# One core, two blocks: the first block's output stage by halves of the tokens, and a new order of products in every half block of weights

## The chip, the cores and the metric

The kernel runs on one core of a Trainium2 chip. The metric is the device time of one execution in microseconds (us), the median of several executions. Five engines work side by side, each through an order of instructions of its own that is fixed when the kernel is built: TensorE (PE in the profile, its weight loads apart as PEld), VectorE (DVE), ScalarE (ACT), GpSimd (POOL) and SyncE (SP), which issues the DMAs.

## The reference, cut to what matters

`x` holds 512 tokens of 2048 channels. A first block (convolution, attention, gates) ends in an output product, a norm and a residual; a second block starts with a norm, a modulation by a vector, and a wide product:

```python
# first block, its end
out = merged @ w_o                                   # 2048 x 2048
x = x + gate * rms_norm(out, g_post)
# second block, its start
h = rmsnorm(x, norm_g) * (1.0 + scale) + shift
u = h @ w_in                                         # 68 blocks of 128 columns, as the kernel lays them out
```

`u` feeds a gated delta network (8 heads) and an RWKV mixer. The same `w_in` is also applied to 256 context tokens, whose mixers run earlier.

## The kernel before

**Layout.** Activations are kept with channels on the partitions: 16 tiles of 128 channels x 512 tokens. A weight block is 128 output columns over 16 slices of 128 input channels. For precision, each operand is held as a pair hi + lo in fp32r (`split`, L104: ACT casts to hi at L105, DVE subtracts at L106 to get lo), and a product of two pairs is three matmuls: hi·hi, hi·lo and lo·hi, the first factor being the weight.

**Products.** `mblock` (L132) makes one block of 128 columns for T tokens in a PSUM bank: it calls `products` (L141) for each half block of 8 slices. `products` loads a half block of weights (512 KB, three buffers `wraw`), splits it into `whi` and `wlo` (two buffers each), and issues 24 matmuls at L157. For each slice k in turn it issues whi·act_hi, whi·act_lo, wlo·act_hi. Four slices instead of eight are taken where tiles of the activation become ready bit by bit.

**Order.** A scheduler puts the instructions of each engine in order when the kernel is built, by their place in the program (the priority) and by when its own model of time has them ready. Within `products`, groups of `K.burst` matmuls (12, later 6) are kept together.

**The output stage** (L1470 to L1491, in `block1`). 16 blocks of `wo` for all 512 tokens; each is scaled out of PSUM by DVE (L1470, tiles `out0` to `out15`), squared by ACT, and the squares are summed by POOL (`ChanSS` with `pe=False`). Then `rinv` sums over the partitions with two matmuls and computes an inverse root in 11 DVE operations (`rsqrt`, L161 to L175). Each of the 16 tiles is scaled by it (L1478, DVE), x is added (L1479, DVE for every third tile, POOL for the others), the sum is stored to DRAM (L1480) and its squares are summed by PE (L290). A second `rinv` follows, and then `modulate_steps` (L335) makes the pairs `h` tile by tile. As soon as four tiles are there, `products` goes through the same four slices of three blocks of the second block's weights (`K.pre`, blocks `B_LO` to `B_LO+2`; `PRE = 3`), which stay in three PSUM banks (`px0`, `px1`, one `pc`). `mixers_gdn` then takes the fourth such block by `mblock` (bank `pd`) and starts the heads.

**Other users of `products`.** The context stage runs `mblock` with T = 256 (tiles `hc`); there POOL makes every second `wlo` (`K.on_pool = 2`). The eight heads of the delta network in `mixers_gdn` take four blocks each with T = 512, `K.burst` = 6.

Of the kernel before, what the change touches and what calls it, by code (L numbers as in the profile page):

```python
# [9 lines left out]
F32 = mybir.dt.float32  # L10
# [3 lines left out]
ALU = mybir.AluOpType  # L14
# [41 lines left out]
PRE = 3  # L56
# [55 lines left out]
class Visit:  # L112
# [6 lines left out]
    def mm(self, *a, **kw):  # L119
# [5 lines left out]
        if self.first:  # L125
            tc.add_manual_dep(i, self.first.name, mybir.DependencyInfo(mybir.DependencyClass.NoSync,
                                                                       mybir.DependencyReason.DATA), reason="visit")
        else:
            self.first = i
# [11 lines left out]
def products(K, ps, wap, act, T, ka, w, k0, k1):  # L141
# [9 lines left out]
    for k in range(w):  # L151
        ah, al = act[k]
        for j, (a, b) in enumerate(((hi, ah), (hi, al), (lo, ah))):
            n = 3 * (ka - k0 + k) + j
            ahead = FIRST if n % K.burst else 0
            tc.cur_priority -= ahead
            nc.tensor.matmul(ps[:, :T], lhsT=a[:, k], rhs=b, start=(n == 0), stop=(n == 3 * (k1 - k0) - 1))  # L157
            tc.cur_priority += ahead
# [1248 lines left out]
def block1(K, h, big, late, cc):  # L1407
# [31 lines left out]
    with left(K, "ext", 16) as ext:  # L1439
# [21 lines left out]
        with right(K, "ot") as op:  # L1461
            K.x1d = K.dram.tile([16, 128, 512], F32, name="x1d")
            outs = []
            ss = ChanSS(K, op, 512, 16, "or", False)
            gg = op.tile([128, 16], F32, name="gg")
            nc.vector.tensor_tensor(gg, K.mod["ada"][:, 32:48, 0], K.v["g_post"], op=ALU.mult)
# [9 lines left out]
            for i in range(16):  # L1476
                x, o = xs[i], outs[i]
                nc.vector.tensor_tensor(o, o, ro, op=ALU.mult)  # L1478
                (nc.gpsimd if i % 3 else nc.vector).tensor_tensor(o, o, x, op=ALU.add)  # L1479
                K.dma.dma_start(K.x1d[i], o)  # L1480
                s2.add(o)
# [365 lines left out]
```

## Time and profile before

| what | value |
|---|---|
| median of 3 executions | 3961.03 us (3956.98 to 3964.54) |
| profiled execution: time | 3948.75 us |
| profiled execution: span | 3947.0 us |
| mean granted TensorE clock in it | 0.962 of full speed |
| PE busy | 3672.7 us (93%) |
| DVE busy | 2748.4 us (70%) |
| ACT busy | 1359.4 us (34%) |
| POOL busy | 505.4 us (13%) |

Times in the rows are us from the start of the span. The busy time of PE counts matmuls that overlap in the pipeline, so where PE is busy all the time its rate is read from the distance between starts.

### The profile page before, as it was taken

What the parts mean: (1) busy time and instruction counts of PE and PEld (TensorE: products, weight loads), DVE (VectorE), ACT (ScalarE), POOL (GpSimd) and SP (SyncE); (2) the same over time, 40 slices, a digit from 0 to 9 for tenths busy, and PEclk for the clock granted to TensorE, in tenths of its full rate; (3) what the DMA queues carried; (4) which work ended last, traced back from release to release, by engine and by line L of the source; (5) the groups of instructions that cost most, each with busy time, mean ns of one, the idle gap of its engine ahead of it and who ended that gap; (6) DMA issues with size and microseconds to landing.
All of it is one profiled execution on the core that took longest, in us unless ns stands there. A gap on an engine that the chain in (4) does not pass through costs nothing. (4 is left out here: it accounts for less than half of the span.)

```text
span 3947.0 us, 81802 instructions
## 1 busy us (share of the span) xinstructions
PE 3672.7 (93%) x33066; PEld 2837.3 (72%) x33066; DVE 2748.4 (70%) x7146; ACT 1359.4 (34%) x2713; POOL 505.4 (13%) x595
## 2 busy tenths in 40 slices
PE   8899878999999999999998889989999999998997
PEld 4577678876777777777886577777877777766676
DVE  3366798788778778553524877776767778877866
ACT  3322333323334344332322432322323444444333
POOL 0100231003101001000311201100001111111102
PEclk9999899999999999999999999999999999999998
DMA  8766445423433333425523222222223122212235
GB/s 321 269 226 216 161 133 173 140 102 127 136 118 107 118 111 126 130 81 179 204 93 129 101 88 68 67 69 75 86 79 110 65 68 81 68 67 83 91 129 203
DMA packets 206491, 492.95 MB, mean 125 GB/s; under 512 B 40096, under 2 KB 71328, under 8 KB 202016
## 3 DMA queue, kind: packets, MB, share of 16 engines
q1 hardware_dynamic: 206112, 487.72, 36.4%
q8 instruction: 260, 4.26, 0.4%
q14 instruction: 119, 0.97, 0.1%
HBM read 434.54 MB, written 53.09 MB: 124 GB/s over the span
## 5 line engine op out<-in xcount | busy, mean ns | idle before, releaser
L157 PE MATMUL pd<-big,whi 128*128 128x512 f32 x5280 | 1759.5, 411 | 8.0 <-ACT big L352 8.0
L157 PEld LDWEIGHTS pd<-big,whi 128*128 128x128 f32 x5280 | 964.4, 192 | 251.4 <-issue 20.8
L157 PE MATMUL pd<-big,wlo 128*128 128x512 f32 x2768 | 1104.2, 399 | 24.3 <-DVE wlo L106 23.6
L105 ACT CAST whi<-wraw 128x1024 fp32r<-128x1024 f32 (+2 forms) x498 | 502.9, 1010 | 1159.5 <-PE pd L157 1074.7
L106 DVE TENSOR_TENSOR wlo<-wraw,whi 128x1024 fp32r<-128x1024 f32 (+2 forms) x478 | 572.9, 1199 | 318.4 <-ACT whi L105 311.2
L157 PEld LDWEIGHTS pd<-big,wlo 128*128 128x128 f32 x2768 | 530.0, 191 | 147.1 <-DVE wlo L106 28.2
L157 PE MATMUL pd<-hc,whi 128*128 128x256 f32 x1152 | 227.0, 297 | 11.5 <-ACT hc L352 5.5
L157 PE MATMUL pd<-hc,wlo 128*128 128x256 f32 x576 | 171.7, 298 | 33.0 <-DVE wlo L106 23.9
L157 PEld LDWEIGHTS pd<-hc,whi 128*128 128x128 f32 x1152 | 188.3, 199 | 15.3 <-ACT hc L352 5.6
L157 PE MATMUL pd<-ext,whi 128*128 128x512 f32 x512 | 184.6, 401 | 3.8 <-DVE ext L106 3.8
L1160 DVE SCALAR_TENSOR_TENSOR cv_y<-cv_up,vec,cv_y 128x512 f32<-128x512 f32 x240 | 180.9, 754 | 4.2
L157 PE MATMUL pd<-fa,whi 128*128 128x512 f32 x448 | 149.9, 414 | 0.9 <-ACT fa L105 0.8
L157 PEld LDWEIGHTS pd<-hc,wlo 128*128 128x128 f32 x576 | 114.8, 199 | 40.0 <-DVE wlo L106 28.0
L944 POOL TENSOR_TENSOR rg_bk<-rg_th,rg_L 64x512 f32<-64x512 f32 x48 | 69.1, 1439 | 400.5 <-ACT rg_L L923 274.0
L1055 ACT ACTIVATE rg_zw<-rg_H,rg_wc 64x64 f32<-64x64 f32 x320 | 102.8, 342 | 43.4 <-DVE rg_H L1077 39.2
L157 PEld LDWEIGHTS pd<-ext,whi 128*128 128x128 f32 x512 | 97.3, 190 | 27.9 <-DVE ext L106 4.7
L1077 DVE SCALAR_TENSOR_TENSOR rg_H<-pc,rg_wc,rg_zw 64x64 f32<-64x64 f32 x320 | 90.4, 282 | 33.7 <-PE pc L123 24.0
L567 DVE SCALAR_TENSOR_TENSOR gc_y<-gc_up,vec,gc_y 128x512 f32<-128x512 f32 (+1 forms) x160 | 108.6, 679 | 2.8 <-issue 0.2
L242 DVE SCALAR_TENSOR_TENSOR ada_ev<-wraw,cs_ada,ada_ev 128x512 f32<-128x512 f32 x120 | 93.7, 781 | 20.3 <-DMA wraw<-in_wada_dram 18.9
L157 PEld LDWEIGHTS pd<-fa,whi 128*128 128x128 f32 x448 | 80.7, 190 | 21.8 <-ACT fa L105 1.9
L157 PE MATMUL pd<-fa,wlo 128*128 128x512 f32 x224 | 89.1, 398 | 0.7 <-DVE wlo L106 0.7
L405 DVE COPY_PREDICATED iv_u<-cpi,px 128x256 f32<-128x256 int32 (+2 forms) x112 | 35.2, 340 | 73.2 <-PE px L402 62.8
(589 smaller groups left out, 5592.9 us busy)
## 6 DMA issues: line engine op xcount, KB each, us to landing
wraw<-in_w_dram SPq DMA_DIRECT2D x366, 512.0 KB, 3.6
wraw<-in_wada_dram SPq DMA_DIRECT2D x128, 512.0 KB, 4.5
wraw<-in_wada_dram SPq DMA_DIRECT2D x32, 1024.0 KB, 4.8
wraw<-in_wo_dram SPq DMA_DIRECT2D x32, 512.0 KB, 3.5
sgl<-sgd SPq DMA_DIRECT2D x48, 256.0 KB, 3.3
wraw<-in_wout_dram SPq DMA_DIRECT2D x20, 512.0 KB, 3.8
wraw<-in_w_dram SPq DMA_DIRECT2D x36, 256.0 KB, 3.6
sgd<-msg SPq DMA_DIRECT2D x32, 256.0 KB, 3.3
```

Of the source, the lines that this page charges most:

```text
L105: K.nc.scalar.copy(hi, src)
L106: (eng or K.nc.vector).tensor_tensor(lo, src, hi.bitcast(F32), op=ALU.subtract)
L157: nc.tensor.matmul(ps[:, :T], lhsT=a[:, k], rhs=b, start=(n == 0), stop=(n == 3 * (k1 - k0) - 1))
L242: nc.vector.scalar_tensor_tensor(ev, raw[:, k], cs[:, kk, 0:1], ev, op0=ALU.mult, op1=ALU.add)
L405: nc.vector.copy_predicated(u32[:, m0:m0 + w], K.cp[d, lev].unsqueeze(1).to_broadcast([128, w, 32]), zp[:, m0:m0 + w])
L567: nc.vector.scalar_tensor_tensor(y, up[:, t:t + T], w[:, t:t + 1], y, op0=ALU.mult, op1=ALU.add)
L944: nc.gpsimd.tensor_tensor(bk[uq, :, u], th[uq], F[uq], op=mul)
L1055: nc.scalar.activation(zw[hv[u], d], H[hv[u], ms[d], u], AF.Copy, scale=wn[hv[u], 4 * d + mn])
L1077: nc.vector.scalar_tensor_tensor(Hn[hv[u], 4 * d + mn, u], pc3[hv[u], 2, d], wn[hv[u], 4 * d + mn], zw[hv[u], d], op0=mul, op1=ALU.add)
L1160: nc.vector.scalar_tensor_tensor(y, up[:, t:t + 512], w[:, t:t + 1], y, op0=ALU.mult, op1=ALU.add)
```

## The change

Four things are changed.

- `products` issues, for a half block, first all whi·act_hi and whi·act_lo of its slices, and then all wlo·act_hi. This holds for every product of the kernel that goes through it.
- The output stage becomes a function of its own, `block1_out`, that works on tokens 0 to 255 and then on tokens 256 to 511. The `wo` products of the first half come first; their norm, residual, second norm and modulation (`norms(0)`) are spread over the `wo` products of the second half, three steps per block. The squares of the second norm are summed by POOL in the first half and by PE in the second; x is loaded in halves with three buffers.
- `PRE` falls away: four blocks instead of three are begun ahead, each in two halves of 256 columns of its bank. The first halves of all four are issued with the steps of `norms(1)` between them, and the second halves follow the modulation of the second half of the tokens.
- A dependency without a wait (`behind`) keeps the second half of a bank after its first half. `Visit` uses the same helper, with no other effect.

All weights of `wo` and of the four blocks are loaded and split twice, once for each half. The hi part of `h` takes the place of the hi part of the merged activations.

```diff
-PRE = 3
...
-def products(K, ps, wap, act, T, ka, w, k0, k1):
+def products(K, ps, wap, act, T, ka, w, k0, k1, after=None):
...
-    for k in range(w):
-        ah, al = act[k]
-        for j, (a, b) in enumerate(((hi, ah), (hi, al), (lo, ah))):
-            n = 3 * (ka - k0 + k) + j
-            ahead = FIRST if n % K.burst else 0
-            tc.cur_priority -= ahead
-            nc.tensor.matmul(ps[:, :T], lhsT=a[:, k], rhs=b, start=(n == 0), stop=(n == 3 * (k1 - k0) - 1))
-            tc.cur_priority += ahead
+    n = 3 * (ka - k0)
+
+    for a, k, b in [(hi, k, b) for k in range(w) for b in act[k]] + [(lo, k, act[k][0]) for k in range(w)]:
+        ahead = FIRST if n % K.burst else 0
+        tc.cur_priority -= ahead
+        i = nc.tensor.matmul(ps[:, :T], lhsT=a[:, k], rhs=b, start=(n == 0), stop=(n == 3 * (k1 - k0) - 1)).ins
+        tc.cur_priority += ahead
+        if after:
+            behind(K, i, after)
+            after = None
+        n += 1
+    return i
...
-            outs = []
-            ss = ChanSS(K, op, 512, 16, "or", False)
...
-            for i in range(16):
-                o = op.tile([128, 512], F32, name=f"out{i}")
-                ps = mblock(K, A["wo"][i], m, 512)
-                nc.vector.tensor_scalar(o, ps, gg[:, i:i + 1], None, op0=ALU.mult)
-                ss.add(ps)
-                outs.append(o)
-            ro = ss.rinv(1.0 / 2048, EPS)
-            s2 = ChanSS(K, op, 512, 16, "or")
-            xs = [loader(K, ext, A["xT"], 512, "ext", 16)(i) for i in range(16)]
...
-            for m in modulate_steps(K, op, lambda k: outs[k], pair_of(big, "big"), r2, 512, "ng2", "ada2", 0, "or"):
-                h.append(m)
-                k = len(h) - 4
-                if k % 4 == 0:
-                    for b, ps in K.pre.items():
-                        products(K, ps, A["w2"][b], h[k:], 512, k, 4, 0, 16)
-            return h
+            return block1_out(K, big, op, m)
+
+
+def block1_out(K, big, op, m):
...
+    outs = [op.tile([128, 512], F32, name=f"out{i}") for i in range(16)]
+    h = [(hi, big.tile([128, 512], F32R, name="big")) for hi, _ in m]
+    hs = [slice(0, 256), slice(256, 512)]
+
+    def wo(t, sums):
+        act = [[x[:, hs[t]] for x in pair] for pair in m]
+        for i in range(16):
+            ps = mblock(K, A["wo"][i], act, 256)
+            nc.vector.tensor_scalar(outs[i][:, hs[t]], ps, gg[:, i:i + 1], None, op0=ALU.mult)
+            sums.add(ps)
+            yield
+
+    def norms(t, sums):
+        ro = sums.rinv(1.0 / 2048, EPS)
+        s2 = ChanSS(K, op, 256, 16, "os", t == 1)
+        get = loader(K, op, A["xT"][:, :, hs[t]], 256, "or_x", 3)
+        yield
+        for i in range(16):
+            x, o = get(i), outs[i][:, hs[t]]
+            nc.vector.tensor_tensor(o, o, ro, op=ALU.mult)
+            (nc.gpsimd if i % 3 else nc.vector).tensor_tensor(o, o, x, op=ALU.add)
+            K.dma.dma_start(K.x1d[i][:, hs[t]], o)
+            s2.add(o)
+            yield
+        r2 = s2.rinv(1.0 / 2048, EPS)
+        yield
+        it = iter(h)
+        yield from modulate_steps(K, op, lambda k: outs[k][:, hs[t]], lambda: [x[:, hs[t]] for x in next(it)], r2, 256,
+                                  "ng2", "ada2", 0, "om")
+
+    sums = ChanSS(K, op, 256, 16, "or", False)
+    run(wo(0, sums))
+    first = norms(0, sums)
+    run(first, 1)
+    sums = ChanSS(K, op, 256, 16, "or", False)
+    for _ in wo(1, sums):
+        run(first, 3)
+    run(first)
+    K.pre = {B_LO + j: p.tile([128, 512], F32, name=n) for j, (p, n) in
+             enumerate(((K.px, "px0"), (K.px, "px1"), (K.pc, "pc"), (K.pc, "pc")))}
+    other = norms(1, sums)
+    done = {}
+
+    def begin(t, k):
+        act = [[x[:, hs[t]] for x in pair] for pair in h[k:k + 4]]
+        for b, ps in K.pre.items():
+            done[b] = products(K, ps[:, hs[t]], A["w2"][b], act, 256, k, 4, 0, 16, done[b] if t and not k else None)
+            if not t:
+                run(other, 1)
+
+    for k in range(0, 16, 4):
+        begin(0, k)
+    run(other, 2)
+    for k in range(0, 16, 4):
+        run(other, 4)
+        begin(1, k)
+    return h
```

## Rows read from the trace of the kernel before

**Rows 1.** The page: busy time of PE, DVE, ACT and POOL in the span.
```profile
PE 3672.7 (93%) x33066; PEld 2837.3 (72%) x33066; DVE 2748.4 (70%) x7146; ACT 1359.4 (34%) x2713; POOL 505.4 (13%) x595
```
**Rows 2.** Stretches: length, busy (count) of PE PEld DVE ACT POOL, clock, DMA, GB/s.
```profile
1969.00:2147.00 178.00, 178.00 (x770) 144.39 (x769) 52.34 (x57) 43.04 (x49) 25.41 (x15) 1.00 0.30 104
2147.00:2194.00 47.00, 20.04 (x35) 5.67 (x34) 41.99 (x48) 11.90 (x19) 18.19 (x11) 0.81 0.34 127
2194.00:2235.00 41.00, 38.62 (x144) 28.91 (x144) 30.40 (x39) 24.69 (x39) 11.18 (x7) 0.89 0.25 88
2235.00:2247.00 12.00, 11.35 (x49) 8.94 (x49) 11.17 (x16) 4.62 (x7) 0.00 (x0) 1.00 0.50 159
```
**Rows 3.** Timeline of PE: first and last `wo` product, first of the second block.
```profile
1968.81 0.39 PE L157 MATMUL pd<-big,whi 128*128 128x512 f32 x1
...
2146.07 0.39 PE L157 MATMUL pd<-big,wlo 128*128 128x512 f32 x1
...
2194.24 1.58 PE L157 MATMUL px<-big,whi 128*128 128x512 f32 x2 [11.15 <-ACT big L352]
```
**Rows 4.** Timeline of DVE: first operations of norm, scaling, second norm, modulation.
```profile
2149.16 0.69 DVE L168 TENSOR_SCALAR or_xh<-po 128x512 f32<-128x512 f32 x1 [1.31 <-PE po L294]
...
2156.89 1.29 DVE L1478 TENSOR_TENSOR out<-out,or_y 128x512 f32<-128x512 f32 x2
...
2183.13 0.69 DVE L168 TENSOR_SCALAR or_xh<-po 128x512 f32<-128x512 f32 x1 [2.19 <-PE po L290]
...
2190.85 2.42 DVE L351 SCALAR_TENSOR_TENSOR or_n<-out,or_gs,or_y 128x512 f32<-128x512 f32 x2
```
**Rows 5.** Timeline of PE, context stage, 256 columns: two starts, 90 products apart.
```profile
639.15 0.28 PE L157 MATMUL pd<-hc,wlo 128*128 128x256 f32 x1
...
649.80 0.28 PE L157 MATMUL pd<-hc,wlo 128*128 128x256 f32 x1
```
**Rows 6.** Groups of instructions, 1975 to 2147: busy, mean ns, idle before.
```profile
L106 DVE TENSOR_TENSOR wlo<-wraw,whi 128x1024 fp32r<-128x1024 f32 x30 | 36.8, 1226 | 63.9 <-ACT whi L105 62.4
L105 ACT CAST whi<-wraw 128x1024 fp32r<-128x1024 f32 x30 | 31.5, 1049 | 123.3 <-PE pd L157 123.3
```
**Rows 7.** Groups of instructions, 2147 to 2220.
```profile
L1478 DVE TENSOR_TENSOR out<-out,or_y 128x512 f32<-128x512 f32 x16 | 19.8, 1283 | 0.0
...
L1479 POOL TENSOR_TENSOR out<-out,ext 128x512 f32<-128x512 f32 x10 | 16.4, 1643 | 25.3 <-DVE out L1478 25.3
...
L106 DVE TENSOR_TENSOR wlo<-wraw,whi 128x512 fp32r<-128x512 f32 x6 | 5.2, 863 | 0.1
```
**Rows 8.** Groups of instructions of 256 columns, 440 to 740 (context stage).
```profile
L173 DVE SCALAR_TENSOR_TENSOR gn_t<-gn_y 128x256 f32<-128x256 f32 x16 | 6.7, 418 | 0.0
...
L347 POOL TENSOR_TENSOR hc_n<-cr_in,c_ri 128x256 f32<-128x256 f32 x7 | 6.2, 883 | 7.6 <-DVE hc L353 7.6
```
**Rows 9.** Waits of PE, 440 to 740: us in total, times, longest.
```profile
PE pd L157 <- DVE wlo L106: 23.9, 16, 4.3
PE pd L157 <- POOL wlo L106: 8.8, 14, 2.0
```
**Rows 10.** A stretch of the context stage, columns as in rows 2.
```profile
548.00:628.00 80.00, 64.44 (x496) 60.53 (x497) 69.04 (x118) 28.45 (x45) 23.92 (x29) 1.00 0.44 150
```
**Rows 11.** Waits of PE, 2396 to 2792 (heads of the delta network).
```profile
PE pd L157 <- DVE wlo L106: 22.6, 5, 4.5
```
**Rows 12.** Timeline of PE around one of these five waits.
```profile
2489.27 0.73 PE L157 MATMUL pd<-big,whi 128*128 128x512 f32 x2
2494.51 0.80 PE L157 MATMUL pd<-big,wlo 128*128 128x512 f32 x1 [4.51 <-DVE wlo L106]
...
2495.96 0.63 PE L157 MATMUL pd<-big,wlo 128*128 128x512 f32 x1
...
2499.80 0.63 PE L157 MATMUL pd<-big,wlo 128*128 128x512 f32 x1
```
**Rows 13.** The stretch of that head, columns as in rows 2.
```profile
2475.00:2555.00 80.00, 74.15 (x765) 60.10 (x764) 58.71 (x184) 23.09 (x42) 8.47 (x21) 0.96 0.21 69
```

More of the change, by code (lines that the diff above doesn't have):

```diff
@@ L125, in mm @@
         if self.first:
-            tc.add_manual_dep(i, self.first.name, mybir.DependencyInfo(mybir.DependencyClass.NoSync,
-                                                                       mybir.DependencyReason.DATA), reason="visit")
+            behind(self.K, i, self.first, "visit")
         else:
@@ L150, in products, with behind @@
     split(K, hi[:, :w], lo[:, :w], raw[:, :w], nc.gpsimd if K.on_pool and K.n_split % K.on_pool == 0 else nc.vector)
-    for k in range(w):
-        ah, al = act[k]
-        for j, (a, b) in enumerate(((hi, ah), (hi, al), (lo, ah))):
-            n = 3 * (ka - k0 + k) + j
-            ahead = FIRST if n % K.burst else 0
-            tc.cur_priority -= ahead
-            nc.tensor.matmul(ps[:, :T], lhsT=a[:, k], rhs=b, start=(n == 0), stop=(n == 3 * (k1 - k0) - 1))
-            tc.cur_priority += ahead
+    n = 3 * (ka - k0)
[9 more added lines that the diff above has]
+    return i
+def behind(K, i, first, reason="order"):
+    K.tc.add_manual_dep(i, first.name, mybir.DependencyInfo(mybir.DependencyClass.NoSync, mybir.DependencyReason.DATA),
+                        reason=reason)
 def rsqrt(K, pool, src, shape, a, eps, name, eng=None, exact=False):
@@ L1473, in block1 @@
-            ro = ss.rinv(1.0 / 2048, EPS)
-            s2 = ChanSS(K, op, 512, 16, "or")
-            xs = [loader(K, ext, A["xT"], 512, "ext", 16)(i) for i in range(16)]
[L1476 to L1481, printed above, removed]
-            r2 = s2.rinv(1.0 / 2048, EPS)
@@ L1483, in block1 @@
-            K.pre = {B_LO + j: p.tile([128, 512], F32, name=n) for j, (p, n) in
-                     enumerate(((K.px, "px0"), (K.px, "px1"), (K.pc, "pc"), (K.pc, "pc"))[:PRE])}
-            h = []
-            for m in modulate_steps(K, op, lambda k: outs[k], pair_of(big, "big"), r2, 512, "ng2", "ada2", 0, "or"):
-                h.append(m)
-                k = len(h) - 4
-                if k % 4 == 0:
-                    for b, ps in K.pre.items():
-                        products(K, ps, A["w2"][b], h[k:], 512, k, 4, 0, 16)
@@ L1492, in block1 @@
-            return h
+            return block1_out(K, big, op, m)
+def block1_out(K, big, op, m):
+    nc, A = K.nc, K.A
+    K.x1d = K.dram.tile([16, 128, 512], F32, name="x1d")
+    gg = op.tile([128, 16], F32, name="gg")
+    nc.vector.tensor_tensor(gg, K.mod["ada"][:, 32:48, 0], K.v["g_post"], op=ALU.mult)
+    outs = [op.tile([128, 512], F32, name=f"out{i}") for i in range(16)]
[50 more added lines that the diff above has]
+    return h
```

3 lines of the change are left out of this document (removed).

## The prediction, made before the changed kernel was run

> **What bounds the kernel now.** I read the page first. PE is busy for 93% of the span, DVE for 70% [rows 1], so only what removes idle or slow time of PE can move the end. The next view was the table of stretches around the output stage [rows 2]. From 1969 to 2147 PE is busy without a gap at full clock. In the 47 us behind it, PE runs 35 matmuls, and DVE is busy for 42.0 us: a chain on DVE sets the pace. In the next 41 us, 144 products of the second block pass, at a mean clock of 0.89, and 12 us later the fourth low-rank block is done. The timelines say which links the chain has: the last `wo` product starts at 2146.07 and the first product of the second block at 2194.24, after a wait for the modulated tile [rows 3]. Between them DVE starts the first inverse root at 2149.16, the scaling at 2156.89, the second root at 2183.13 and the modulation at 2190.85 [rows 4].
>
> The view of waits says where else PE waits for what the change touches. In the context stage it waits 30 times, 32.7 us in all, for a low weight product's operand [rows 9]. In the heads it waits five times, 4.5 us each [rows 11]. One of these in the timeline [rows 12]: two whi products at 2489.27, then nothing until `wlo` is there at 2494.51. The nine products from 2495.96 to 2499.80 start 0.427 us apart, nearly twice the 0.231 us of [rows 3] (177.26 us over 767 intervals). [...]
>
> **Part 1, the halved `wo` products.** 768 products of 512 columns become 1536 of 256. In the context stage 256 columns cost 10.65 us for 90 products, 0.118 us each [rows 5]. 1536 x 0.1183 = 181.7 us against 768 x 0.2311 = 177.5 us: **+4 us**.
>
> Weight loads as the limit: each matmul in [rows 2] has a load of its own (770 and 769), and in [rows 5] a product with its load starts every 0.118 us, so the load is hidden at 256 columns too. [...]
>
> The weights must come twice as fast: one half block per 24 x 0.118 = 2.84 us. The cast takes 1.05 us and the subtraction 1.23 us [rows 6], in sequence 2.3, so both fit. With the old order the `whi` buffer would be held almost to the end of the 24 products; with hi first it is free after 16 of them (0.95 us earlier), and `wlo` is wanted 1.7 us later (14 products). That is what keeps a half block fed at 2.84 us.
>
> The second half of `wo` (90.9 us) also carries `norms(0)`. DVE's work in it: 32 subtractions x 1.226 = 39.2 us, 16 evictions = 7 us (an estimate, 0.6 of their 512-column time), two roots of 11 x 0.42 us = 9.2 us [rows 8], 22 scalings and additions of 0.4 us = 9 us, and the modulation, 11 us (an estimate from the root's 0.42 us per operation): 76 us. POOL has 28 sums of squares, 10 additions and 8 scalings of 0.88 us [rows 8], 41 us. Below, nothing: 76 < 91. Above: DVE and POOL hold each other up, since the scaling takes 1.283 us in the mean beside POOL's additions [rows 7] where DVE's root needs 0.70 us per operation [rows 4]. If they took turns throughout, 76 + 41 = 117 us, 26 us over. SP's queue is in order as well: 16 loads of x (three buffers, so each waits for an addition three tiles back) and 16 stores now stand between weight loads, and a late addition delays the weights behind it. I take **+10 us**, nearer the low end because the three weight buffers lie ahead; range 0 to 26.
>
> **Part 2, what follows `wo`.** Before: from 2146.07 to 2247, when four low-rank blocks are done, 101 us. After, only the second half's chain follows, with 256 columns. DVE's 256-column operation takes 0.418 us [rows 8] against 0.70: ratio 0.6; POOL's 0.883 against 1.643 us [rows 7]: 0.54. Up to the first root 3.1 us become 2.5. The root, 7.7 us, becomes 4.7. Scaling, addition and the sum of squares, 26.2 us, become 15. The second root 4.7. The modulation with the second halves of the products: PE needs 192 x 0.118 = 22.7 us, DVE some 12 us of modulation and 16 subtractions of 0.69 to 0.86 us [rows 7]; I take 28. Sum 55. Meanwhile the first halves of the four blocks (22.7 us of PE work) cover the chain; their 16 subtractions (11 to 14 us) share DVE with it: +7. Total 62 us. Lower bound: PE's work alone, 45.4 us plus 16 sums, 52. Upper: all 14 us of subtractions in the way and a half-clock start, 73. Gain **39 us**, range 28 to 49. This is also the cover of Part 1: the first half's norm and modulation cost nothing because 91 us of products run over them; without that cover they cost what the second half's do, some 40 us.
>
> **Part 3, low products last, elsewhere.** Context stage: `wlo` is wanted 14 x 0.118 = 1.7 us later and `whi` is free 0.95 us earlier, against a mean wait of 32.7/30 = 1.1 us. By that nearly all 32.7 us go. But in a stretch where PE is busy for 64.4 of 80 us, DVE is for 69.0 [rows 10]: it can be shortened by no more than 11 us before DVE is the limit, and it is in order. I take **-10 us**, range 0 to 33.
>
> [...] I take **-20 us**, range 0 to 35.
>
> The rest of the kernel shows PE waits for `wlo` of under 1 us each, so no gain; but the scheduler lays the whole order out anew. I price that at 0, with 12 us to either side, the size of the profiled run's distance from the median. The fourth bank (`pc`) is held until the low-rank step reads it, as the other three are: 0.
>
> **Sum.** +4 + 10 - 39 - 10 - 20 = -55 us. Against the profiled time, 3948.75 - 55 = 3894. That run lies 12.3 us below the median, so the median should be 3906; I say **3907 us**.
>
> **The rivals.**
> - *Only the order gains.* `wo`'s second half is paced by DVE and POOL (+26) and the chain ends at its upper bound (-28): +2 with the 4 us. Then 3961 - 30 + 2 = 3933. For it: DVE's 42.0 of 47 us [rows 2]. Against it: nine tenths of that chain move under products that run anyway. 0.12.
> - *Only the halves gain.* DVE sets the pace in the context stage and the heads, so the waits only move: 3961 - 25 = 3936. For it: [rows 10]. Against it: [rows 13]. 0.07.
> - *More than forecast*: Part 3 near its bounds (-33 and -35) with Part 1 and 2 as taken: 3961 - 25 - 68 = 3868. 0.09.
> - *No change that can be seen*: losses of the first rival with no gain from the order: 3963. 0.09.
> - *Slower*: in the second half of `wo`, loads of x and stores in SP's queue hold the weights back. The context stretch shows such a pace, 496 matmuls in 80 us, 0.161 us each [rows 10]: 768 products x 0.161 = 124 us, +33; with the chain at -28, +4, and nothing from Part 3, +9 over before: 3970. It decides from about 0.16 us per product with no gain elsewhere; if the order gains its 30 us, from 0.20 us on. [...] A 256-column product at the cost of a 512-column one (hidden loads failing) would give 1536 x 0.231 = 355 us, 4080 in the end; [rows 5] leave it 0.01. Together 0.09.
>
> **How the numbers follow.** The forecast itself, with all three parts at work, has 0.54 and runs from 3880 to 3932. Faster by over 0.2% (7.9 us, about what a measurement of this kernel can tell from no change): forecast, more, only order, only halves, 0.82. Within it 0.09, slower 0.09. The range takes in both one-sided rivals and the larger gain: **3866 to 3960**.
>
> **What would show it.** `wo` products without gaps, about 0.118 us apart, for 182 to 192 us; PE idle behind `wo` for under 15 us instead of most of 47; four low-rank blocks done some 62 us after it; no wait of 4.5 us for `wlo` in the heads, at most 1.5 us, and no half clock behind it; context waits for `wlo` under 15 us. The prediction is wrong if the second half of `wo` takes over 115 us, if the chain behind it is over 75 us, or if the heads keep 80 us each.

## The result, and the profile after

The changed kernel takes 4009.12 us (median of 4, 3999.21 to 4022.77) against 3962.78 us (median of 4): ratio 1.0127, 95% interval 1.0085 to 1.0169. It is **46 us slower**; the forecast was 55 us faster, 3907 us, with 3960 us as its upper end.

The profiled execution has a span of 4021.0 us at a mean granted clock of 0.947; the one of before had 3947.0 us at 0.962 [rows 1]. The page's first row, after:

```profile
PE 3736.3 (93%) x34034; PEld 2932.2 (73%) x34034; DVE 2798.4 (70%) x7284; ACT 1420.0 (35%) x2819; POOL 531.9 (13%) x641
```

To see where the time went, I cut both executions at the issue of the same DMAs: the end of the context stage's first part, the end of the mixers that follow, the last load of attention's gate (just ahead of `wo`), the low-rank store behind the output stage, and the first store of the mixer that follows the heads. The view of stretches for the last four parts (attention; output stage; gates and heads; the second mixer to the end), before, columns as in [rows 2]:

```profile
1144.00:1962.80 818.80, 797.67 (x6671) 602.62 (x6671) 535.06 (x1374) 298.73 (x654) 67.77 (x50) 0.99 0.40 134
1962.80:2250.50 287.70, 257.71 (x1039) 195.96 (x1038) 141.97 (x165) 89.09 (x118) 57.09 (x34) 0.95 0.31 110
2250.50:3022.60 772.10, 722.04 (x6789) 585.77 (x6789) 558.98 (x1682) 232.91 (x414) 74.28 (x168) 0.96 0.25 81
3022.60:3947.00 924.40, 848.24 (x11156) 642.54 (x11156) 707.95 (x1987) 373.95 (x901) 134.31 (x121) 0.94 0.28 94
```

The same stretches of the changed kernel:

```profile
1147.20:1987.30 840.10, 813.26 (x6670) 612.23 (x6670) 535.94 (x1374) 301.21 (x655) 65.34 (x50) 0.97 0.40 130
1987.30:2280.20 292.90, 261.55 (x2014) 251.19 (x2013) 187.19 (x296) 140.07 (x224) 81.80 (x80) 0.97 0.54 180
2280.20:3069.10 788.90, 735.54 (x6818) 596.96 (x6817) 571.44 (x1707) 237.45 (x418) 84.19 (x172) 0.95 0.25 79
3069.10:4021.00 951.90, 876.45 (x11124) 660.40 (x11122) 697.16 (x1971) 372.86 (x898) 127.57 (x117) 0.91 0.28 92
```

The output stage, where the halves were to gain 25 us, is 5 us longer. The other three are 21, 17 and 28 us longer, and their clock is lower. In the attention and the second mixer only the order of products is changed; in the heads' part 10 of the 17 us are a wait that the output stage leaves behind it (the last rows of this section). In the two earlier parts the differences are 1.8 us less and 5 us more.

**Most waits for `wlo` are gone all the same.** The view of waits of PE, context stage (438 to 738), after, answers [rows 9], 32.7 us before:

```profile
PE pd L154 <- DVE wlo L105: 6.7, 3, 3.4
```

In the heads (2430 to 2930) the five waits of [rows 11] have no successor; the longest list entries are now

```profile
PE px L404 <- issue: 5.6, 5, 1.2
PE pc L122 <- DVE gd_vn L763: 4.4, 6, 0.8
PE po L845 <- ACT go_t L1138: 2.7, 2, 1.5
```

**The output stage.** Stretches of the changed kernel: `wo`'s first half, its second half in five pieces, and the stretch behind it, up to the last of the four low-rank blocks:

```profile
1993.60:2085.00 91.40, 91.40 (x775) 91.24 (x774) 47.28 (x58) 39.84 (x49) 17.12 (x15) 1.00 0.54 187
2085.00:2097.00 12.00, 12.00 (x101) 11.83 (x100) 11.59 (x24) 3.91 (x5) 2.73 (x1) 1.00 0.48 163
2097.00:2121.00 24.00, 16.47 (x119) 15.46 (x119) 13.85 (x21) 10.49 (x20) 19.22 (x22) 0.93 0.59 187
2121.00:2145.00 24.00, 21.83 (x181) 21.52 (x181) 18.28 (x26) 11.26 (x19) 7.86 (x9) 1.00 0.73 246
2145.00:2169.00 24.00, 21.21 (x161) 20.40 (x160) 22.49 (x38) 17.55 (x33) 11.25 (x11) 0.93 0.43 151
2169.00:2194.60 25.60, 25.60 (x220) 25.60 (x219) 12.06 (x13) 10.57 (x14) 4.41 (x4) 1.00 0.49 166
2194.60:2273.40 78.80, 61.89 (x421) 55.90 (x420) 53.30 (x106) 37.79 (x76) 17.16 (x18) 0.91 0.49 156
```

The first half runs at 91.4/775 = 0.118 us per product, with a load for each. The second half, with the first half's norms beside it, loses its time mostly in two places: 119 matmuls in the 24 us from 2097 and 161 in the 24 us from 2145, where some 204 fit (181 in the 24 us between them). `wo` takes 201 us in all against 177.7, and the stretch behind it 78.8.

The first of the two places on ACT (timeline, last item: what ended the idle time): between two casts of weights stand a square `or_sq` of the next `wo` block and squares `os_sq` of the norm.

```profile
2104.93 1.03 ACT L104 CAST whi<-wraw 128x1024 fp32r<-128x1024 f32 x1
2109.17 0.38 ACT L296 ACTIVATE or_sq<-pd 128x256 f32<-128x256 f32 x1 [3.21 <-DVE out L1489]
2110.69 0.42 ACT L296 ACTIVATE os_sq<-out 128x256 f32<-128x256 f32 x1 [1.14 <-DVE out L1501]
2112.24 0.42 ACT L296 ACTIVATE os_sq<-out 128x256 f32<-128x256 f32 x1 [1.13 <-POOL out L1501]
2113.61 0.42 ACT L296 ACTIVATE os_sq<-out 128x256 f32<-128x256 f32 x1 [0.95 <-POOL os_acc L304]
2113.93 1.03 ACT L104 CAST whi<-wraw 128x1024 fp32r<-128x1024 f32 x1
```

Two casts, 9.0 us apart; PE needs one per 2.84 us. ACT is idle for 6.4 us between them: 3.2 end with DVE's scaling of the `wo` block, 2.3 with additions of DVE and POOL, and 0.95 with a sum of POOL (`os_acc`) that frees one of the two buffers of `os_sq`. The second place is DVE's: busy for 22.49 of 24 us, with the modulation among its subtractions.

Behind `wo`, SP's timeline shows one thing that the norm of the second half waits for (e4 below tests whether it sets the pace): x comes in groups of three, each behind three stores of the tiles before (`x1d`), with weights between, and a group takes some 6 us.

```profile
2214.54 1.40 SPq L1281 DMA_DIRECT2D or_x<-in_xT_dram  x3
2216.04 0.85 SPq L146 DMA_DIRECT2D wraw<-in_w_dram  x2
2219.79 1.29 SPq L1502 DMA_DIRECT2D x1d<-out  x3
2221.18 1.37 SPq L1281 DMA_DIRECT2D or_x<-in_xT_dram  x3
```

And a wait that the forecast did not have, of PE for the gates' inverse, early in the heads' part; before and after:

```profile
PE px L518 <- DVE gg_R L488: 6.4, 1, 6.4
PE px L526 <- DVE gg_R L496: 16.3, 1, 16.3
```

### The profile page after: what moved, and what is told of

Read it like the earlier page. It is cut to its first block, busy times and chain, and to the rows that moved or that the text cites. A ratio compares the mean times of both kernels' runs of the same rounds, so it can differ in the third digit from the quotient of the medians.

```text
span 4021.0 us, 84357 instructions
## 1 busy us (share of the span) xinstructions
PE 3736.3 (93%) x34034; PEld 2932.2 (73%) x34034; DVE 2798.4 (70%) x7284; ACT 1420.0 (35%) x2819; POOL 531.9 (13%) x641
## 4 chain that ended last, share of the span: by engine, by line
PE 73%; DVE 14%; DMA 5%; issue 3%; ACT 3%; POOL 2%; SPq 0%; DVEq 0%; ACTq 0%; POOLq 0%
PE pd L154 51%; PE pc L122 4%; DVE wlo L105 2%; PE px L1000 2%; PE po L122 1%; PE po L245 1%; DMA wraw<-in_wada_dram 1%; PE po L1223 1%; PE px L410 1%; PE px L404 1%; PE po L323 1%; PE po L845 1%; DMA cr_in<-in_ctxT_dram 1%; PE px L978 1%; PE px L154 1%
## 5 line engine op out<-in xcount | busy, mean ns | idle before, releaser
L154 PE MATMUL pd<-big,whi 128*128 128x512 f32 (+1 forms) x5504 | 1472.4, 401 | 19.7 <-ACT whi L104 8.5
L154 PEld LDWEIGHTS pd<-big,whi 128*128 128x128 f32 x5504 | 1028.9, 194 | 261.7 <-issue 26.0
L105 DVE TENSOR_TENSOR wlo<-wraw,whi 128x1024 fp32r<-128x1024 f32 (+2 forms) x528 | 619.0, 1173 | 301.3 <-ACT whi L104 132.0
L154 PE MATMUL pd<-big,wlo 128*128 128x512 f32 (+1 forms) x3008 | 746.3, 383 | 3.8 <-DVE wlo L105 3.7
L154 PE MATMUL pd<-ext,whi 128*128 128x256 f32 (+1 forms) x768 | 190.7, 324 | 3.8 <-DVE ext L105 3.8
L154 PE MATMUL pd<-hc,whi 128*128 128x256 f32 x1152 | 169.4, 300 | 8.0 <-ACT hc L360 5.2
L154 PEld LDWEIGHTS pd<-ext,whi 128*128 128x128 f32 x768 | 148.4, 193 | 16.9 <-DVE ext L105 4.3
L1063 ACT ACTIVATE rg_zw<-rg_H,rg_wc 64x64 f32<-64x64 f32 x320 | 102.5, 342 | 50.4 <-DVE rg_H L1085 40.6
L154 PE MATMUL pd<-hc,wlo 128*128 128x256 f32 x576 | 83.5, 289 | 6.8 <-DVE wlo L105 6.7
L1000 PE MATMUL px<-rg_C,rg_bk 64*128 64x128 f32 x512 | 86.3, 305 | 1.1 <-ACT rg_bt L979 0.6
L386 DVE TENSOR_TENSOR iv_sh<-iv_sh,iv_n 128x64 f32<-128x64 f32 (+2 forms) x336 | 80.9, 241 | 6.4
```

The source lines that it names most:

```text
L105: (eng or K.nc.vector).tensor_tensor(lo, src, hi.bitcast(F32), op=ALU.subtract)
L154: i = nc.tensor.matmul(ps[:, :T], lhsT=a[:, k], rhs=b, start=(n == 0), stop=(n == 3 * (k1 - k0) - 1)).ins
L386: nc.vector.tensor_tensor(sh, sh, n8[:, :, i:i + 1].to_broadcast([128, w, 8]), op=ALU.mult)
L1000: nc.tensor.matmul(pg[:, m], lhsT=bk[q, 4 * r + m].rearrange("p x c -> p (x c)"), rhs=C[q, 4 * r + m, u], start=True, stop=True, tile_posi ...
L1063: nc.scalar.activation(zw[hv[u], d], H[hv[u], ms[d], u], AF.Copy, scale=wn[hv[u], 4 * d + mn])
```

## The experiments

Each run lists span and mean granted clock of every execution. In the traces of before and of the changed kernel the granted clock has two values, full and half: their 86 and 118 records are all at 1.0 or 0.5. Span times clock is the time that the execution would take if its half-clock time took half as long; the table gives its mean over the executions of a run ("full clock"), and span times (1 - clock) as "at the clock". The sum stands for span, 1.8 us below the device time. Within one kernel the first hardly moves (before: 3801.6 us with a standard deviation of 3.8 over 124 executions), so it is used here to ask whether a version has less to do and wait for, or only a better clock. It is a measure, not a proof: it counts half-clock time in which PE is idle too (of the 47 us from 2147 in [rows 2], at 0.81, PE is busy for 20). In the profiled executions before has 296 us at half clock, with PE busy in 224 of them; e1 has 369 and 297, the changed kernel 428 and 352. The idle part stays near 72 to 76 us, so what grows is work of PE at half clock.

The ratios are to executions of before taken beside each run, whose medians lie between 3956 and 3967 us; the first row is over all of them.

| run | edit | median us | ratio to before, 95% | full clock | at the clock |
|---|---|---|---|---|---|
| before | | 3962.2 | | 3801.6 | 159 |
| after | the change | 4009.1 | 1.0127 (1.0085 to 1.0169) | 3805.8 | 202 |
| e1 | order alone | 3989.2 | 1.0061 (1.0038 to 1.0083) | 3791.7 | 196 |
| e2 | halves alone | 3985.0 | 1.0056 (1.0035 to 1.0077) | 3821.4 | 163 |
| e3 | halves, order at 256 columns | 3982.2 | 1.0048 (1.0021 to 1.0075) | 3812.6 | 171 |
| e4 | after, x ahead | 4013.2 | 1.0124 (1.0093 to 1.0155) | 3807.3 | 206 |
| e5 | e4, pieces of eight slices | 4013.8 | 1.0146 (1.0111 to 1.0182) | 3805.0 | 208 |
| e6 | e1, one low product first | 3969.9 | 1.0014 (0.9994 to 1.0033) | 3793.7 | 172 |
| e7 | e1, low last per four slices | 3969.6 | 1.0018 (1.0000 to 1.0037) | 3788.2 | 178 |
| e8 | e5, order at 256 columns | 3972.8 | 1.0034 (1.0011 to 1.0057) | 3804.9 | 166 |
| e9 | before, order at 256 columns | 3966.8 | 1.0016 (0.9999 to 1.0033) | 3790.8 | 174 |
| e10 | e8, two norm steps per `wo` block | 3968.7 | 1.0018 (0.9998 to 1.0037) | 3801.7 | 165 |
| e11 | e10, three blocks ahead | 3955.6 | 0.9980 (0.9964 to 0.9996) | 3796.6 | 158 |
| e12 | e8, first half's squares on PE | 3979.3 | 1.0047 (1.0028 to 1.0066) | 3801.9 | 176 |
| e13 | before, order in the heads | 3965.3 | 1.0011 (0.9993 to 1.0029) | 3787.0 | 174 |
| e14 | e13, groups of three there | 3951.4 | 0.9985 (0.9966 to 1.0005) | 3788.4 | 163 |
| e15 | e1, old order in the heads | 3983.1 | 1.0060 (1.0038 to 1.0083) | 3789.3 | 192 |
| e16 | e11 and e14 | 3963.5 | 0.9997 (0.9981 to 1.0012) | 3792.5 | 169 |
| e17 | before, groups of three in the heads | 3948.2 | 0.9964 (0.9948 to 0.9980) | 3785.3 | 161 |
| e18 | e1, groups of three at 512 columns | 4000.2 | 1.0096 (1.0063 to 1.0130) | 3805.5 | 194 |

### Which of the two parts loses (e1, e2, e3)

e1 is before with the new loop of `products`; e2 is after with the old order; e3 is after with

```diff
+    order = [(hi, k, b) for k in range(w) for b in act[k]] + [(lo, k, act[k][0]) for k in range(w)]
+    if T == 512:
+        order = [x for k in range(w) for x in ((hi, k, act[k][0]), (hi, k, act[k][1]), (lo, k, act[k][0]))]
```

> The kernel before with the new order of products alone (all whi products of a half block, then all wlo), no halves. Theory A (the new order itself costs: it lets the scheduler lay out the rest anew, PE's small matmuls stand together and the clock falls more often): 3985 to 4010 us, half-clock time well over the 298 us of before. Theory B (the halved output stage costs, the order is neutral or gains): 3925 to 3965 us.

> The changed kernel with the old order of products (whi, whi, wlo slice by slice) everywhere, so the halves alone. Theory A: 3950 to 3980 us, the five waits of 4.5 us back in the heads and the attention stage as long as before. Theory B: 4000 us or more.

> The changed kernel with the new order only where a product has 256 columns (context stage, output stage, begun blocks), the old order for 512 columns. Theory A: 3945 to 3970 us, since the layout of attention, heads and RWKV is that of the old order. Theory B: 3995 us or more, as the changed kernel.

Both lose, by 24 and 22 us, and the two add up to the change's 46 to 50. e1 lies in theory A's range, e2 and e3 between the ranges of both theories. By the measure above they lose in different ways. The halves alone add 20 us of work and waits and leave the clock nearly where it was. The order alone *gains* 10 us at full clock and loses 37 to the clock. Attention and second mixer in e1, then output stage and heads' part in e2:

```profile
1144.30:1979.10 834.80, 806.11 (x6671) 606.55 (x6670) 536.47 (x1375) 302.25 (x655) 65.42 (x50) 0.98 0.41 131
3042.20:3979.50 937.30, 865.85 (x11124) 653.16 (x11122) 696.96 (x1971) 374.45 (x898) 127.45 (x117) 0.93 0.29 93
1971.90:2266.50 294.60, 264.39 (x2004) 250.71 (x2003) 193.89 (x295) 139.71 (x223) 84.88 (x80) 0.97 0.57 179
2266.50:3048.90 782.40, 724.74 (x6792) 587.57 (x6792) 566.54 (x1691) 234.04 (x415) 74.27 (x168) 0.96 0.26 80
```

The profiles say how far a stage of one execution can be trusted. In twelve of them PE has the attention's 6668 matmuls in one and the same order, the old one, and takes 818 to 830 us for them; in five with the new order (after, e1, e4, e5, e15) it takes 832 to 840. For the second mixer it is 924 to 930 us in seven profiles with the order of before, and 937 to 952 in four with that of e1. So e1's order does cost time in both stages (e15, whose heads keep the old order, has 926.5 us in the second mixer), and a difference of 10 us in one stage of one profile shows little by itself.

### The halves, repaired step by step (e4, e5, e8, e10, e12, e11)

e4 loads the second half's x into 16 tiles of `ext`, free behind the last `wo` product; e5 takes the first halves of the four blocks in two pieces of eight slices; e8 is e5 with e3's order.

```diff
+        if t:
+            xs = [ext.tile([128, 512], F32, name="ext")[:, :256] for i in range(16)]
+            for i in range(16):
+                K.dma.dma_start(xs[i], A["xT"][i, :, hs[t]])
+            get = lambda i: xs[i]
...
-    for k in range(0, 16, 4):
-        begin(0, k)
+    for k in range(0, 16, 8):
+        begin(0, k, 8)
```

> The changed kernel, but x of the second half of the tokens is loaded into sixteen tiles of the pool that the merged activations leave, instead of three tiles in turn. If the round trips of x through three buffers set the pace behind the last wo product (32 us from the scaling to the second root), that stretch falls to about 16 us and the kernel to 3992 to 4000 us; if DVE or POOL set it, 4005 to 4012 us as the changed kernel.

> e4_x_ahead, and the first halves of the four low-rank blocks go in two pieces of eight slices (512 KB, 24 products) instead of four pieces of four (256 KB, 12 products). If the three weight buffers pace the first halves (16 pieces in about 30 us instead of 22.7 us of products, with the sums of squares queued behind them on PE), the stretch from the last wo product to the first modulated product falls from 47 us to about 38 us and the kernel to about 4000 to 4006 us. If not, both stay.

> e5_eight with the new order only for products of 256 columns (as e3_order_256). If the cost of the order at 512 columns and that of the output stage add up, this lies below e3_order_256 by what e5_eight gains in the chain, at 3965 to 3975 us: about the kernel before. Rival: the low-rank step and the gates behind take the gain back and it stays at 3980 us or more.

The stretch behind `wo` became shorter, 79 to 75 (e4) to 71 us (e5), yet neither run is faster than the changed kernel, nor shorter by more than 1 us at full clock; where the saving went is not shown. Beside the old order at 512 columns (e8, in its forecast range, against e3) x and pieces are worth 8 us at full clock.

e4's expectation had 16 us from the scaling to the second root if x's round trips set the pace. It is 29.9 us (32.6 in the changed kernel), so they were not what held the root. With x ahead the last addition is done by 2217, and the sums of squares still come one tile at a time, with twelve products of the first halves between them on PE (e4: DVE's first scaling and second root, then PE):

```profile
2200.09 0.76 DVE L1505 TENSOR_TENSOR out<-out,or_y 128x256 f32<-128x256 f32 x2
...
2229.97 0.42 DVE L176 TENSOR_SCALAR os_xh<-po 128x256 f32<-128x256 f32 x1
```

```profile
2217.19 0.59 PE L298 MATMUL po<-os_sq,cst 128*128 128x256 f32 x2
2217.43 1.30 PE L154 MATMUL pc<-big,whi 128*128 128x256 f32 x8
2218.57 0.64 PE L154 MATMUL pc<-big,wlo 128*128 128x256 f32 x4
2219.05 0.59 PE L298 MATMUL po<-os_sq,cst 128*128 128x256 f32 x2
```

With three blocks begun ahead instead of four the same stretch is 22.8 us (e11 below, against 29.6 in e10).

The next three each take one suspect of what is left: e10 thins the first half's norms out, e12 takes POOL's sums out of them, and e11 is e10 with the fourth block begun behind the others in one piece, as before (the norm's steps beside the first halves are then three per piece instead of two).

```diff
     for _ in wo(1, sums):
-        run(first, 3)
+        run(first, 2)
```
```diff
-        s2 = ChanSS(K, op, 256, 16, "os", t == 1)
+        s2 = ChanSS(K, op, 256, 16, "os")
```
```diff
-             enumerate(((K.px, "px0"), (K.px, "px1"), (K.pc, "pc"), (K.pc, "pc")))}
+             enumerate(((K.px, "px0"), (K.px, "px1"), (K.pc, "pc")))}
```

> The last version of the halves (x ahead, pieces of eight slices, new order at 256 columns alone: 3972.8 us, wo products 200 us from first to last, the second half 109 us of it) with two steps of the first half's norms per block of wo instead of three. Theory S: the second half is held up because 16 squares with two buffers tie ACT's casts to POOL's sums while three tiles per block pass; thinner, 8.5 us per three tiles against the round trip of some 5.7 us, the stall around the tenth to twentieth microsecond goes and wo takes 183 to 190 us; 3958 to 3963 us. Rival D: DVE has too much to do in that half, wherever it stands: wo stays at 197 to 201 us, 3970 to 3976 us.

> The last version of the halves (3972.8 us, three steps per block) with the first half's squares summed by PE too, as the second half's are, so that POOL has 14 sums less and the two buffers of squares are freed by PE. Theory S: the stall goes, since nothing ties the casts to POOL's additions of squares: wo's second half 109 us down to 95 to 100, with 16 sums of some 0.4 us added to PE (6 us); 3962 to 3970 us. Rival X, that loads of x (three buffers, behind the stores in SP's queue) set the pace of the tiles and the weights behind them: the second half stays at 107 to 112 us, 3972 to 3980 us. Rival D (DVE): no change in the stall either.

> The same with three blocks begun ahead instead of four; the fourth follows in one piece of 512 columns as in the kernel before, while DVE and ACT make the gates. Theory G: the fourth block begun ahead took away the products that covered the gates' chain (PE waited 6.4 us for it before and 15 to 16 us in the versions with halves; from the first low-rank step to the first head it is 8 us longer). With it back, PE's wait is 6 to 8 us and this run is 6 to 9 us faster than the one with four, so about 3951 to 3956 us if theory S holds, the first version of the halves below the kernel before. Rival: the fourth block costs 11.4 us of PE where it stands, whatever is above it, and the halves gave that away elsewhere already: same as the run with four to within 3 us.

e10: `wo` in 196.5 instead of 201 us (e8), where theory S had 183 to 190 and rival D 197 to 201. Thinner norms ease the first of the two places; the second remains, so neither theory holds alone. Halves of `wo` in e10:

```profile
1974.50:2066.00 91.50, 91.37 (x773) 91.07 (x771) 46.99 (x57) 40.93 (x49) 17.98 (x15) 1.00 0.54 185
2066.00:2171.00 105.00, 96.19 (x773) 93.67 (x773) 81.02 (x120) 53.24 (x88) 47.62 (x46) 0.98 0.60 200
```

The same 773 matmuls take 13.5 us longer with the norms beside them. In e12 PE's waits for `whi` and `wlo` fell from 9.6 to 2.7 us, as S has it, but PE waits 6.6 us for the squares instead, and its 16 sums are added: `wo` takes 204 us, its second half 113 where S had 95 to 100. POOL's sums had a part in holding the casts; that they were the cause of the stall is not shown, and PE is the wrong place for them.

e11 bears theory G out: the gates' wait, 15.6 us in e10, is back to

```profile
PE px L529 <- DVE gg_R L499: 5.4, 1, 5.4
```

the heads' part is 773.0 us instead of 782.7, and the run is 13 us faster than e10 and 7 us faster than the kernel before. The fourth block, left as one piece of 512 columns behind the others, is what covers the gates' chain on DVE.

### The order (e9, e13, e15, e6, e7, e14, e17, e18, e16)

e9 has it in the context stage alone, e13 in the delta network's function alone, e15 everywhere else.

> The kernel before with the new order in products of 256 columns alone, so in the context stage and nowhere else. If the order's loss sits at 512 columns (the reading so far: the first part of the context stage was 5 us shorter in the run with the order alone, attention, heads and the last product 13, 17 and 9 us longer), this gives 3954 to 3958 us, ratio 0.9985, and the stages from the attention on are as before to within 3 us. Rival, that any new order costs by relaying the whole program: 3965 to 3985 us, with the later stages longer although their own products are not touched. My forecast of -10 us for this stage alone would give 3950.

> The kernel before with the new order inside the delta network's function alone (all at 512 columns, 24 products kept in groups of six). Theory L, that the loss of the heads is made there: PE's waits for wlo go, the small matmuls of the heads stand apart from the products and some run at half the clock, and the stretch from the first head's output to the seventh's is 480 to 486 us instead of 467: ratio 1.004, 3973 to 3980 us. Theory W, that it comes from the earlier stages, whose changed order lays the whole program out anew: the heads stay at 467 to 470 us and the run is like the kernel before, 3956 to 3966 us. My forecast: 20 us faster.

> The new order everywhere but in the delta network's function. By theory L the heads are back at 467 to 470 us and what remains of the order's 24 us is the attention's 13 and the last product's 9 us less the context's 5: 3968 to 3976 us, ratio 1.003. By theory W the heads are still 478 to 486 us and the run is as slow as with the order everywhere, 3980 to 3990 us.

At full clock e9 gains 10.8 us (forecast for the context stage 10) and e13 14.6 (for the heads 20). Both give it back at the clock, 15 us each, and the time is that of before within the intervals. e9's 3966.8 us is in its rival's range, but not for the rival's reason: PE has the attention and the second mixer in the order of before. In the stages themselves the gain does not show as time: the context stage's two parts are 2.5 us shorter in e9's profile, and the heads' part in e13, from the low-rank store to the next mixer, is 782.0 us at 0.95 against 772.1 at 0.96. From the first head's output to the seventh's it is, before and in e13,

```profile
2413.10:2880.60 467.50, 435.83 (x4498) 354.80 (x4498) 342.64 (x1070) 134.53 (x243) 45.70 (x110) 0.97 0.22 75
2410.20:2895.50 485.30, 463.22 (x4562) 377.66 (x4561) 347.26 (x1093) 143.02 (x252) 49.39 (x112) 0.95 0.22 73
```

18 us longer, as theory L had it (480 to 486), though the five waits of 4.5 us are gone and only 64 matmuls more fall into it (484.9 us in e1's profile); the time of the whole run is theory W's. The view of groups in the heads of before shows the small matmuls at full clock:

```profile
L123 PE MATMUL po<-gd_egt,S 128*128 128x128 f32 x96 | 18.6, 275 | 0.0
L123 PE MATMUL po<-gd_at,gd_vn 128*128 128x128 f32 x96 | 18.5, 275 | 0.0
```

and in e13 each is longer in the mean, and some wait where none did:

```profile
L124 PE MATMUL po<-gd_at,gd_vn 128*128 128x128 f32 x96 | 21.7, 313 | 1.4 <-DVE gd_vn L758 1.4
L124 PE MATMUL po<-gd_egt,S 128*128 128x128 f32 x96 | 21.5, 311 | 0.0
```

In the changed kernel such a stretch lies between 2572 and 2596. PE is busy for 21 of the 24 us, at half the clock throughout; the stretch before it has 279 matmuls at full clock:

```profile
2550.00:2572.00 22.00, 20.56 (x279) 15.70 (x265) 12.73 (x38) 6.68 (x15) 1.57 (x6) 1.00 0.30 91
2572.00:2596.00 24.00, 21.13 (x82) 18.61 (x83) 11.97 (x46) 4.46 (x10) 4.32 (x8) 0.50 0.07 23
```

It holds eight big products and 74 small matmuls; the two small groups here take 434 and 421 ns where they took 275:

```profile
L122 PE MATMUL po<-gd_at,gd_vn 128*128 128x128 f32 x12 | 4.0, 434 | 0.7 <-DVE gd_vn L763 0.7
L154 PE MATMUL pd<-big,whi 128*128 128x512 f32 x8 | 3.9, 641 | 0.0
L122 PE MATMUL po<-gd_egt,S 128*128 128x128 f32 x12 | 3.8, 421 | 0.0
```

I read this so: products that no longer wait for `wlo` run earlier and together, and the small matmuls that used to stand between them are left to themselves. That is argued from such stretches, not shown. e15 shows that the heads are not where most of it is lost: with the old order there the run is as slow as e1, with an attention of 832.2 us in its profile.

Variants of the order: e6 issues `[(lo, 0, act[0][0])]` first in each half block, so that the hi products wait for `wlo` again; e7 applies the new order to groups of four slices.

> e1_order_only, but each half block begins with one wlo product, then all whi products, then the other wlo products. Theory A1 (the new order costs because a half block may start before wlo is there, which lets the scheduler move products away from the small matmuls): 3960 to 3972 us, as before, and half-clock time near 298 us. Theory A2 (any new layout of the order costs some 20 us, or the order inside a half block itself does): 3980 to 3995 us as e1_order_only, half-clock time near 371 us.

> e1_order_only with the low products last in each four slices instead of each eight (8 whi, 4 wlo, 8 whi, 4 wlo). Theory A1: between before and e1_order_only, 3970 to 3982 us, with the heads' 4.5 us waits partly back (6 of 14 products gained). Theory A2: anywhere from 3955 to 3995 us with no order between before, this and e1_order_only.

Both take back most of the loss, at the clock (172 and 178 against 196 us), and keep the gain at full clock. In e6 PE's waits for `wlo` on DVE are back (50.4 us in all, 6.7 in e1) and the time is still shorter than e1's, so a removed wait is not worth its length here. In their profiles the attention (817.6 and 818.5 us) and the second mixer (924.1 in both) are as before, and the heads' part (790.0 and 793.8) is longer than e1's 777.9: theory A1 holds for the run and not for every stage.

A count from the traces tests my reading. Of the attention's matmuls outside `products`, 48 begin at half clock before, 206 in e15, 200 in e1, 230 in the changed kernel, and 61 and 58 in e6 and e7, as the reading has it. But e11, whose attention PE runs in the order of before, has 190 (and 830.3 us); in the heads it is 46 before, 188 in e13 and 186 in e17, which is the fastest of all; and in the second mixer it is `products` themselves whose number grows (82 before, 123 in e1, 176 in the changed kernel), not the others (725, 730, 691). So the count goes with the clock, and what makes the clock fall stays open.

Groups: e14 sets `K.burst = 3` in the delta network's function of e13, e17 does so in the kernel before, e18 in the attention, the heads and the second mixer of e1, and e16 joins e11 and e14.

> The same with groups of three products instead of six in the heads, so that the scheduler may put small matmuls between the products more often. Theory L with groups as its cause: the heads come back to 465 to 473 us, 3955 to 3966 us. If what matters is only that the 16 hi products can go before wlo exists, smaller groups change little: 478 to 488 us, 3970 to 3982 us.

> The kernel before with groups of three in the delta network's function and the old order. If smaller groups alone gained what the run with order and groups of three gained over the one with groups of six (14 us), this gives 3942 to 3950 us. If the groups matter only together with the new order, whose 16 hi products can be cut into pieces without waiting for wlo: 3954 to 3964 us, as before, with the five waits of 4.5 us for wlo still there.

> The run with the order alone (1.0061) with groups of three instead of six in the attention, the heads and the mixer after them. Theory P: the order loses because its products go in a bunch and leave the small matmuls of the attention, the heads and the mixer to themselves, at half the clock or idle; groups of three let them in, so half-clock time comes back (mean clock 0.954 to 0.959 or more) and the run to 3950 to 3966 us. Rival T, that what counts is when the scheduler's model has the operands ready, not the size of a group: still 3975 to 3990 us.

> The best version of the halves (three blocks, thin, x ahead, new order at 256 columns: 0.998 of before) with the new order in groups of three in the delta network's function, which by itself gave 0.9985. If the two gains are apart they add: ratio 0.9965, 3944 to 3950 us, below both kernels. Rival: the second is only another layout of the later stages (there the last product's stage differed by 8 us between two runs that had the same code for it), which the halves lay out anew anyway: 0.998 to 1.000.

e14 is faster than either of its theories had it. e17 is the fastest version of all, 0.9964, with one number changed and the old order; at full clock it gains 16 us. Its waits for `wlo` in the heads, against [rows 11], and its stretch from the first head's output to the seventh's:

```profile
PE pd L157 <- DVE wlo L106: 1.5, 3, 0.9
```

```profile
2400.10:2866.90 466.80, 446.52 (x4548) 363.91 (x4545) 343.93 (x1080) 137.96 (x249) 43.92 (x108) 0.97 0.24 75
```

So the five waits of 4.5 us came with groups of six, and the theory that they would stay in e17 was wrong. But the stretch is no shorter than before's 467.5 us without them, and the heads' part is 773.1 against 772.1: that the gain lies in the heads is not shown (the profiled execution, of 3952.8 us, is slower than that of before). In e18 the attention is 821.8 us (834.8 in e1, 818.8 before), but 327 of its matmuls now run in the part ahead of it, which is 8 us longer than in e1; the two together take 1338.0 us (1342.9 in e1, 1325.5 before). The part behind the heads grows to 954.9 us (937.3 in e1, 924.4 before). The run is slower than both theories had it: the size of the groups isn't the cause everywhere, and theory P falls. The gains of e11 and e14 do not add (e16), as its rival said.

## Why the prediction was wrong, point by point

**Part 1, +14 us taken, +23 measured.** The 4 us for 256 columns are right: 91.4 us for the first half, with 774 loads beside its 775 products, so the loads are hidden at 256 columns, as forecast. The second half was forecast at 101 us and took 109.6. The sum of DVE's work, 76 us, was below the half, and it was nearly all there (11.6 + 13.9 + 18.3 + 22.5 + 12.1 = 78 us busy). What failed is the step from sums to time. The work is not spread evenly: additions and squares came in one bunch, among ACT's casts, and the modulation in another. The bounds (0 to 26) held it: 10 + 9 = 19.

**Part 2, 62 us forecast, 78.8 measured.** The first root starts at 2196.50, 2 us after `wo`; its operations take 0.42 us each, as taken, but with five subtractions among them it needs 7.7 us and not 4.7, and scaling begins at 2204.22. Scaling, addition and squares were put at 15 us and took 2204.22 to 2236.80, 32.6 us. The step that failed is the overlap: the first halves of the four blocks were to cover the chain at a price of 7 us for DVE, and 15 us came from the ratio of 512 to 256 columns on DVE and POOL alone. But PE takes the sums of squares one tile at a time between pieces of these first halves, so the chain goes at the pace of PE's products (29.9 us with x ahead in e4; 29.6 in e10 and 22.8 with one block less in e11). The new loads of x with three buffers, queued behind stores, were priced in Part 1 and not here; they add 2.7 us (32.6 against 29.9). With x ahead and bigger pieces (e5) the whole is 71 us, inside the forecast's range of 52 to 73.

**Not in the forecast at all: the cover of the fourth block.** I priced the fourth bank at 0 because of its buffer. It was the block's products that mattered: 11 us of PE work that hid the gates' chain. Moved ahead, they leave a wait of 16.3 instead of 6.4 us (e11 against e10 shows it alone).

**Part 3, -30 forecast, +24 measured (e1).** The first step is right: the waits went, and at full clock e9 and e13 gain 10.8 and 14.6 us. The steps that failed are that a removed wait is worth its length, and that the half clock behind it goes with it (in before 0.50 from 2495.96 to 2499.80, behind the wait of [rows 12]). The 20 us for the heads were my estimate and no run shows them: without the five waits the stretch that holds the heads is 18 us longer in e13, at 0.95 instead of 0.97; e9 and e13 as a whole take the time of before. I priced the clock only behind the waits that I removed, and took the rest of the kernel at 0 with 12 us to either side. By the measure above the clock took 37 us in e1. By the stretches of its profile attention is 16 us longer than before (834.8), the part behind the heads 13 (937.3) and the heads' part 6 (777.9). The forecast had nothing on the first two: they had no wait for `wlo` of note, and it did not ask what the order does to the work between the products.

**The rivals.** *Slower* had 0.09, with 3970 us and a single place. Its mechanism, weights held up in the second half of `wo`, is there, at 0.143 us per product (109.6/768) and not 0.16, and by itself it does not make 46 us. Two of the prediction's own signs of being wrong came: the chain is over 75 us, and the heads keep some 80 us each (485.3 us for six in e13).

**The sum.** Halves: -25 forecast, +22 measured, 47 us off, of which about 9 lie in the second half of `wo`, 17 in the chain, and 10 in the lost cover; the last 11 were not located (e2's profile has 9 us in the three parts ahead of the output stage, no more than the spread between executions). Order: -30 forecast, +24 measured, 54 off.

**What stays open.** Why the clock falls more with the new order, where the gain of e17 lies, and why groups of three harm the second mixer (e18) was not settled: an edit to the heads also changes the order that the scheduler gives the second mixer, whose code it doesn't touch. Why the clock takes back what the context stage alone gains (e9) is open too.

## What to carry to other kernels

Don't price a removed wait at its length: ask what will then run where, and at which clock. Here some 50 us of waits went (e1) and the kernel was 24 us slower. When a stage is halved to hide its chain, list each work that the old stage covered (here the gates) and each queue that the new pieces pass one after the other (sums behind products, casts behind squares), and not only the busy sums. Try the knob beside the code first: the group size in the heads alone gave 0.36%, where the whole change lost 1.3%. And hold a stage of one profile against the same stage in other profiles with the same order before reading 10 us into it.

## What the runs showed of the hardware

- Executions of one and the same kernel differ mostly by the clock. Before had spans from 3938.6 us at 0.965 to 3980.3 us at 0.955; times clock both are 3801 us.
- PE's busy share does not tell it here: 93% before and after, at 0.962 and 0.947. Small matmuls keep PE "busy" for 21 of 24 us at half the clock (above).
- In the first half of `wo` a weight load is hidden behind every product of 256 columns: 775 matmuls and 774 loads in 91.4 us.
